# The first block of the FFN's up-projection: another order for the second token pair's sums and for the work left over at its end

## The chip, the core and the metric

One core of one Trainium2 chip runs the whole kernel as one program. The metric is the device time of that program in microseconds (us), as the median of several runs. The engines named below are PE (TensorE, the matrix products), DVE (VectorE), ACT (ScalarE), POOL (GpSimd) and SP (SyncE, which here issues nearly all DMAs). Matrix products write into PSUM, which has eight banks; DVE and ACT read the banks, POOL does not.

## The reference, cut to what matters

A trunk of two layers over 1040 tokens (16 learned ones in front of 1024) of width 1024. Layer 0 has an SSD mixer, layer 1 a stick-breaking attention. Behind each stands the same convolutional, gated FFN, and the change lies in the first half of that FFN, in both layers:

```python
def _conv_ffn(u, w_up, conv_w, conv_b, w_down):
    h = _causal_dwconv(u @ w_up, conv_w, conv_b)   # 3 taps along the tokens
    g, val = jnp.split(h, 2, axis=-1)
    return (jax.nn.silu(g) * val) @ w_down          # D_FF = 2816
```

All is float32. The kernel keeps that precision by splitting each operand into a high and a low part and making three matrix products of each one.

## The kernel before, in words

**Products.** `mm3` (line 206) issues three matmuls for one 128-row step: high by high (line 209), low by high (line 210), high by low (line 211). The up-projection takes 128 gate columns and the 128 value columns that belong to them as one *block* `b`; there are 22 blocks. The tokens form four tiles of 260 (layer 0) or 256 (layer 1), taken as two *pairs*: `block(b, 0, ...)` is the first pair, `block(b, 1, ...)` the second. For one block and one pair, gate and value columns, two halves of the width and two token tiles make a two-by-two by two-by-two product, which is done with seven products instead of eight. Each of the seven takes a *form* of the tokens (a sum or difference of token tiles and halves, made once per layer by `forms`, line 1080) and a form of the weights (made per block by `up_weights`, line 1172). One product is four steps of `mm3`, twelve matmuls.

**Where the sums stand.** Products 0 and 1 share a bank of the tag `mm` (2 banks; for the first pair of block 1 the single bank of the tag `ex`), called `x`. Products 2, 4 and 6 add up in a bank of the tag `sm` (3 banks), called `y`. Products 3 and 5 are made in a bank of `lg` (2 banks) or `ex`, called `z`. Between the products, copies of a bank into SBUF (ACT, line 1245: `p1` of `x`, `u2` of `y`, `p5` of `z`) and additions (DVE, the lambda `add`, line 1256) make the four wanted results: `x` is the gate of one tile, the value sum `v1` is the value of the other tile, `z` the gate of that one, `y` the value of the first. Product 6 adds onto `y` and has to wait until the value sum, which reads `y` with product 4 in it, is done. `conv` (line 332) makes the three taps: one ACT instruction (line 336) and two DVE instructions (line 339), the two DVE ones on one output one behind the other. `Silu` is an ACT instruction (line 1237), the product of gate and value is made on DVE (line 1241), and SP stores it (line 1242).

**The first block is special.** `enter_ffn` (line 968) makes the token forms of the first pair while the products in front still run, and those of the second pair (`rest`, the second half of `forms`) while PE already works on block 0. So block 0 is staggered: PE does the first pair's products and, between them, the second pair's products 0 and 1; products 2, 3, 5 and 4 of the second pair follow as DVE delivers the low parts of their forms (line 1103). On DVE the taps of block 0 are tied behind `first_low` (lines 1190 and 1191), the low part of block 1's first weights, and `first_low` is tied behind `last_low`, the last low part of the forms. A tie made with `behind` (line 200) only fixes the order of two instructions on one engine. What the first pair of block 0 has to do on DVE and ACT is kept in the list `late` and run when the forms are through; the second pair (`early`) runs its own at once, in the order of the source: the two additions onto `z`, the gate, product 4, the value sum `add(p5, p5, y)`, the value, and then product 6.

**Order on the engines.** Around the up-projection no order is written out by hand. A planner places the instructions by their place in the source and a simulated time, within the dependencies and the ties; tiles are taken from pools with a fixed number of buffers. From block 1 on, the two pairs go step by step side by side (`zip(s, t)`), in the order of products 0, 2, 3, 1, 4, 5, 6. Block 1's weights: `f1` (products 0 and 1) has its low part made on DVE as `first_low`, in two halves; `f2` (products 2 and 3), `f4` (product 6) and `f3` (products 4 and 5) have theirs made on POOL (line 102), in that order.

Of the kernel before, what the change touches and what calls it, by code (L numbers as in the profile page):

```python
# [10 lines left out]
AF = mybir.ActivationFunctionType  # L11
# [18 lines left out]
HB = 2  # L30
# [29 lines left out]
KF = FF // P  # L60
# [45 lines left out]
class Trunk:  # L106
# [93 lines left out]
    def behind(self, ins, other, reason):  # L200

        if other is not None:
            nosync = mybir.DependencyInfo(mybir.DependencyClass.NoSync, mybir.DependencyReason.DATA)
            self.tc.add_manual_dep(ins.ins, other.ins.name, nosync, reason=reason)

    def mm3(self, out, wh, wl, uh, ul, first, last, joins=False, tie=None):

# [124 lines left out]
    def conv(self, ps, out, n, taps, halo, wcol, bcol, between=lambda: None, tie=None):  # L332

        nc = self.nc
        o = halo - taps + 1
        nc.scalar.activation(out, ps[:, o : o + n], AF.Identity, scale=wcol(0), bias=bcol)  # L336
        between()
        for i in range(1, taps):
            ins = nc.vector.scalar_tensor_tensor(out, ps[:, o + i : o + i + n], wcol(i), out, op0=ALU.mult, op1=ALU.add)  # L339
            self.behind(ins, tie, "behind the forms")  # L340
        self.last_tap = ins
# [871 lines left out]
    def up(self, layer, w0, forms, rest, pool):  # L1213

        nc = self.nc
        tt = nc.vector.tensor_tensor
        FN = FFN[layer].tile
        N = HB + FN
        cw, cb = f"ffn_conv_w{layer}", f"ffn_conv_b{layer}"
        d = self.dp.tile([KF, P, FFN[layer].n], F32, tag=f"g{layer}", name=f"g{layer}")  # L1220

        def block(b, t, w, late=None, early=False):

            def product(i, ps, start=True):
                wh, wl, c0 = w[i]
                for k in range(KD // 2):
                    c = slice(c0 + k * P, c0 + k * P + P)
                    self.mm3(ps[:, :N], wh[:, c], wl[:, c], *forms[t][0][i][k], start and k == 0, k == KD // 2 - 1, not start, None if k else self.after_sums if late is not None and i else self.first_block if b == 1 else None)  # L1230
                return ps

            def conv(x, i, c):
                o = self.tmp("c")
                self.conv(x, o[:, :FN], FN, 3, HB, lambda q: self.par(cw, (KF * i + b) * 3 + q), self.par(cb, KF * i + b), tie=self.first_low if early or late is not None else None)
                if i == 0:
                    nc.scalar.activation(o[:, :FN], o[:, :FN], AF.Silu)
                return o

            def done(g, v, j):  # L1240
                self.last_up = tt(g[:, :FN], g[:, :FN], v[:, :FN], op=ALU.mult)
                nc.sync.dma_start(d[b, :, FN * j : FN * j + FN], g[:, :FN])

            def copy(ps, s):
                nc.scalar.activation(s[:, :N], ps[:, :N], AF.Copy)  # L1245
                return s

            def gate():
                made.update(g0=conv(x, 0, 0))

            def value():
                if late is not None:
                    self.behind(add(p5, p5, u3), self.first_low, "behind the forms")
                made.update(v1=conv(v1, 1, 1))

            add = lambda o, x, y: tt(o[:, :N], x[:, :N], y[:, :N], op=ALU.add)  # L1256
# [12 lines left out]
            u2 = copy(y, s2)  # L1269
            yield  # L1270
            s3, s4 = pair(late is not None)
            z = product(3, (self.ex if next(turn) else self.lg)("p"))
            p5 = copy(z, s3)
            if early:
                yield
                z = product(5, self.sm("p"))
                yield
                for f in (u2, p5):
                    self.behind(add(z, z, f), self.first_low, "behind the forms")
                gate()  # L1280
            else:
                add(z, z, u2)
                yield
                product(1, x, False)
                run(gate)
                yield
            product(4, y, False)
            if early:
                add(p5, p5, y)
                v1 = p5  # L1290
            elif late is None:
# [6 lines left out]
            if not early:  # L1298
                product(5, z, False)
            run(lambda: done(conv(z, 0, 1), made["v1"], 2 * t + 1))  # L1300
            yield
            product(6, y, False)
            run(lambda: done(made["g0"], conv(y, 1, 0), 2 * t))
            yield

        turn = chain((0, 0, 0, 0), cycle((1, 0, 0)))
        for b in range(KF):
            made = second if b == 1 else self.up_weights(layer, b, pool)
            w = list(made)[-1] if b else w0
            late = [] if b == 0 else None  # L1310
            s, t = block(b, 0, w, late), block(b, 1, w, early=b == 0)
            if b:
                for _ in zip(s, t):
                    pass
            else:
# [798 lines left out]
```

## Time and profile before

| | |
|---|---|
| time, median of 3 runs | 2847.6 us (2846.33 to 2847.69) |
| the profiled execution's own time | 2845.67 us |
| its span, first to last instruction | 2844.0 us |
| PE, DVE, ACT, POOL busy | 99%, 70%, 55%, 55% of the span |
| PE's granted clock, mean | 0.997 |
| entrance of the up-projection, layer 0 | from about 827 us (first product) to about 880 us (last product of block 1) |
| entrance of the up-projection, layer 1 | the same steps, about 1316.6 us later |

Times in the trace are counted from the span's first instruction. A row of the timeline shows the start, the duration, the engine, the source line, the operation, what it writes and reads, how many instructions are merged into the row, and, in brackets, how long the engine stood idle before it and what ended that. Matmuls overlap, so a matmul's duration is longer than the distance to the next one; the distance is the pace. The granted clock is 1.00 at full speed.

### The profile page before, as it was taken

The numbers are of one execution on the slowest core, as the hardware profiler recorded it, in microseconds if no ns is written. First come the engines' busy times: TensorE is split into PE (matmuls) and PEld (weight loads), VectorE is DVE, ScalarE is ACT, GpSimd is POOL, SyncE is SP. The second block draws the span as 40 slices with busy tenths as digits, with TensorE's granted clock in tenths as the row PEclk, the third lists the DMA queues.
The fourth block names the chain that finished last, engine by engine and source line by source line (L and its number), as shares of the span: only waits on it lengthen the run. The fifth ranks groups of instructions, "written<-read, shape, count | busy, mean of one in ns | idle before, by whom it ended". The sixth has DMA issues, their size and how long they took to land.

```text
span 2844.0 us, 56386 instructions
## 1 busy us (share of the span) xinstructions
PE 2803.4 (99%) x21239; PEld 2687.8 (95%) x21239; DVE 2001.7 (70%) x3922; ACT 1554.4 (55%) x2983; POOL 1552.3 (55%) x2144
## 2 busy tenths in 40 slices
PE   8999999999999999999999999999999999999998
PEld 7999999999999999999999999999898999999888
DVE  5676666668486565657886888888758565656776
ACT  5555454543255555555335777777636555555433
POOL 2365555553528777767763121111354787876881
PEclk9999999999999999999999999999999999999999
DMA  4333333343412222235142222222542222225331
GB/s 120 86 113 112 102 85 125 116 137 102 116 68 92 81 77 81 77 120 179 53 149 79 78 66 73 82 70 57 173 145 82 83 75 82 75 83 185 112 104 67
DMA packets 141740, 281.77 MB, mean 99 GB/s; under 512 B 16308, under 2 KB 71741, under 8 KB 141469
## 3 DMA queue, kind: packets, MB, share of 16 engines
q1 hardware_dynamic: 135844, 267.01, 29.6%
q0 software_dynamic: 2048, 6.49, 0.6%
q10 hardware_dynamic: 3576, 4.67, 0.5%
q8 instruction: 168, 2.75, 0.4%
q14 instruction: 104, 0.84, 0.1%
HBM read 207.79 MB, written 55.42 MB: 93 GB/s over the span
## 4 chain that ended last, share of the span: by engine, by line
PE 89%; DVE 7%; ACT 2%; issue 1%; POOL 0%; DMA 0%; DVEq 0%; ACTq 0%; SPq 0%; POOLq 0%
PE p L209 10%; PE p L211 10%; PE p L210 10%; PE acc L209 8%; PE acc L211 8%; PE acc L210 8%; PE pj L209 7%; PE pj L210 7%; PE pj L211 7%; DVE kp L1713 2%; PE po L1759 2%; PE lg L1702 2%; PE wT L1736 2%; PE y L815 1%; PE S L804 1%
## 5 line engine op out<-in xcount | busy, mean ns | idle before, releaser
L102 POOL TENSOR_TENSOR wl<-w,wh 128x256 fp32r<-128x256 f32 x760 | 679.3, 924 | 333.6 <-ACT wh L196 213.4
L209 PE MATMUL pj<-uh,wh 128*128 128x348 f32 (+2 forms) x1536 | 501.5, 327 | 3.8 <-DVE xbc L339 1.6
L210 PE MATMUL pj<-ul,wh 128*128 128x348 f32 (+2 forms) x1536 | 495.2, 322 | 0.2 <-DVE ul L320 0.2
L211 PE MATMUL pj<-uh,wl 128*128 128x348 f32 (+2 forms) x1536 | 492.0, 320 | 0.0
L339 DVE SCALAR_TENSOR_TENSOR c<-p,params,c 128x260 f32<-128x260 f32 (+1 forms) x700 | 325.9, 482 | 132.1 <-ACT c L336 129.0
L210 PE MATMUL p<-bl,fh 128*128 128x262 f32 (+1 forms) x1408 | 399.4, 284 | 1.7 <-DVE bl L1103 1.6
L211 PE MATMUL p<-bh,fl 128*128 128x262 f32 (+1 forms) x1408 | 399.9, 284 | 0.0
L209 PE MATMUL p<-bh,fh 128*128 128x262 f32 (+1 forms) x1408 | 399.6, 284 | 0.0
L102 POOL TENSOR_TENSOR fl<-x,fh 128x256 fp32r<-128x256 f32 x352 | 259.3, 770 | 219.1 <-ACT fh L1186 219.1
L209 PEld LDWEIGHTS pj<-uh,wh 128*128 128x128 f32 x1536 | 288.8, 188 | 8.3 <-DVE qs L1654 3.6
L209 PE MATMUL p<-bh,wh 128*128 128x262 f32 (+1 forms) x1040 | 295.7, 284 | 0.0
L210 PE MATMUL p<-bl,wh 128*128 128x262 f32 (+1 forms) x1040 | 294.7, 283 | 0.0
L211 PE MATMUL p<-bh,wl 128*128 128x262 f32 (+1 forms) x1040 | 294.7, 283 | 0.0
L210 PEld LDWEIGHTS pj<-ul,wh 128*128 128x128 f32 x1536 | 289.5, 188 | 1.7 <-DVE ul L320 0.6
L211 PEld LDWEIGHTS pj<-uh,wl 128*128 128x128 f32 x1536 | 289.0, 188 | 0.1
L210 PEld LDWEIGHTS p<-bl,fh 128*128 128x128 f32 x1408 | 266.9, 190 | 4.4 <-DVE bl L1103 4.1
L209 PEld LDWEIGHTS p<-bh,fh 128*128 128x128 f32 x1408 | 266.8, 190 | 0.1
L211 PEld LDWEIGHTS p<-bh,fl 128*128 128x128 f32 x1408 | 265.9, 189 | 0.0
L336 ACT ACTIVATE c<-p,params 128x260 f32<-128x260 f32 (+1 forms) x350 | 195.0, 559 | 79.2 <-DVE p L1256 53.1
L210 PE MATMUL acc<-gl,wh 128*128 128x260 f32 (+1 forms) x672 | 214.2, 320 | 0.0
L211 PE MATMUL acc<-gh,wl 128*128 128x260 f32 (+1 forms) x672 | 213.4, 319 | 0.0
L1256 DVE TENSOR_TENSOR p<-p,ft 128x262 f32<-128x262 f32 (+1 forms) x174 | 75.9, 436 | 192.2 <-ACT ft L1245 132.3
(340 smaller groups left out, 7556.0 us busy)
## 6 DMA issues: line engine op xcount, KB each, us to landing
w<-in_w_up SPq DMA_DIRECT2D x88, 512.0 KB
w<-in_w_down SPq DMA_DIRECT2D x44, 512.0 KB
w<-in_w_in SPq DMA_DIRECT2D x40, 512.0 KB
E<-ea_d SPq DMA_DIRECT2D x32, 464.0 KB
D<-acs_d SPq DMA_DIRECT2D x32, 420.5 KB
g<-c SPq DMA_DIRECT2D x88, 130.0 KB
g<-c SPq DMA_DIRECT2D x88, 128.0 KB
b<-g SPq DMA_DIRECT2D x16, 520.0 KB
```

Of the source, the lines that this page charges most:

```text
L102: done.append(eng.tensor_tensor(out[:, c], x[:, c], y[:, c], op=op))
L209: self.behind(mm(out, wh, uh, start=first, stop=False, skip_group_check=joins), tie, "behind the sums of squares")
L210: mm(out, wh, ul, start=False, stop=False, skip_group_check=joins)
L211: self.last_mm = mm(out, wl, uh, start=False, stop=last, skip_group_check=joins)
L336: nc.scalar.activation(out, ps[:, o : o + n], AF.Identity, scale=wcol(0), bias=bcol)
L339: ins = nc.vector.scalar_tensor_tensor(out, ps[:, o + i : o + i + n], wcol(i), out, op0=ALU.mult, op1=ALU.add)
L804: nc.tensor.matmul(ps, bk[:n], xde[:n].rearrange("p h d -> p (h d)"), start=True, stop=True)
L1256: add = lambda o, x, y: tt(o[:, :N], x[:, :N], y[:, :N], op=ALU.add)
L1702: nc.tensor.matmul(ps[:nt, a, :m], part[:, c0 : c0 + nt], ks[a][:, s0 : s0 + m], start=x == 0, stop=x == 1)
L1713: nc.vector.tensor_tensor_scan(rev, rev, self.one[:nt].to_broadcast([nt, m + 1]), init, ALU.mult, ALU.mult)
L1736: nc.tensor.transpose(pt[:ns, x * CB : x * CB + nt], bt[:nt, a, x * CB : x * CB + ns], self.ident[:nt, :nt])
L1759: nc.tensor.matmul(po[64 * a : 64 * a + 64, t0:n], v[: CH[c][1], c, 64 * a : 64 * a + 64], wt[a][q][: CH[c][1], r, t0:n], start=x == 0, st ...
```

## The change

Four things, all in `up` and all for block 0 and block 1 alone; the instructions and the arithmetic stay the same, and only their order and one buffer change.

1. The second pair of block 0 now puts its leftovers into a list as well (`late` is a pair of lists). Its value sum goes into a buffer of its own, `s4` (`add(v1, p5, y)`), is tied directly behind the forms' last low part and becomes the new `last_low`; `first_low` is therefore tied behind it. Product 6 follows at once, ahead of all taps of block 0.
2. The second pair's two additions onto `z`, its gate, value and both ends move to the leftovers. The `Silu` of the gate in `x` moves, in both pairs, from the gate's step to the step that finishes that tile (`soften` in `first_done`).
3. Block 1 makes products 0 and 1 of both pairs ahead of product 2 (four products in the two banks `ex` and `mm`), and its first three steps are tied one behind the other on PE.
4. The leftovers of block 0 are placed behind block 1's product 0, in this order (pair, step): the first pair's gate between the two pairs' product 0; then the first pair's first end, the second pair's gate and first end, the first pair's value and second end, the second pair's value and second end.

```diff
+                if b == 1 and i < 3:
+                    self.first_block = self.last_mm
                 return ps
...
+                return soften(o) if i == 0 and soft else o
+
+            def soften(o):
+                nc.scalar.activation(o[:, :FN], o[:, :FN], AF.Silu)
                 return o
...
-            if early:
+            if early or b == 1:
                 product(1, x, False)
                 yield
...
-                for f in (u2, p5):
-                    self.behind(add(z, z, f), self.first_low, "behind the forms")
-                gate()
+                product(4, y, False)
+                v1 = s4
+                self.last_low = self.behind(add(v1, p5, y), self.last_low, "behind the forms")
+                product(6, y, False)
+                self.first_block = self.last_mm
+                late += [gate, value, second_done, first_done]
+                yield
+                return
...
+            def first_done():
+                if late is not None:
+                    soften(made["g0"])
+                done(made["g0"], conv(y, 1, 0), 2 * t)
...
+            def second_done():
+                if early:
+                    for f in (u2, p5):
+                        self.behind(add(z, z, f), self.first_low, "behind the forms")
+                done(conv(z, 0, 1), made["v1"], 2 * t + 1)
...
+                next(t)
                 second = self.up_weights(layer, 1, pool)
                 next(second)
-                while late:
-                    for f in late[:2]:
-                        f()
-                    del late[:2]
-                    next(t, None)
-                for _ in t:
-                    pass
+            else:
+                s, t = block(b, 0, w), block(b, 1, w)
+                if b == 1:
+                    next(s)
+                    late[0][0]()
+                    next(t)
+                    for i, n in ((0, 3), (1, 0), (1, 3), (0, 1), (0, 2), (1, 1), (1, 2)):
+                        late[i][n]()
+                for _ in zip(s, t):
                     pass
-                self.first_block = self.last_mm
```

More of the change, by code (lines that the diff above doesn't have):

```diff
@@ L204, in behind @@
             self.tc.add_manual_dep(ins.ins, other.ins.name, nosync, reason=reason)
+        return ins
     def mm3(self, out, wh, wl, uh, ul, first, last, joins=False, tie=None):
@@ L1230, in product, with conv @@
                     self.mm3(ps[:, :N], wh[:, c], wl[:, c], *forms[t][0][i][k], start and k == 0, k == KD // 2 - 1, not start, None if k else self.after_sums if late is not None and i else self.first_block if b == 1 else None)
+                if b == 1 and i < 3:
+                    self.first_block = self.last_mm
                 return ps
-            def conv(x, i, c):
+            def conv(x, i, c, soft=True):
                 o = self.tmp("c")
-                self.conv(x, o[:, :FN], FN, 3, HB, lambda q: self.par(cw, (KF * i + b) * 3 + q), self.par(cb, KF * i + b), tie=self.first_low if early or late is not None else None)
-                if i == 0:
-                    nc.scalar.activation(o[:, :FN], o[:, :FN], AF.Silu)
+                self.conv(x, o[:, :FN], FN, 3, HB, lambda q: self.par(cw, (KF * i + b) * 3 + q), self.par(cb, KF * i + b), tie=self.first_low if b == 0 else None)
+                return soften(o) if i == 0 and soft else o
+            def soften(o):
+                nc.scalar.activation(o[:, :FN], o[:, :FN], AF.Silu)
                 return o
@@ L1248, in gate @@
             def gate():
-                made.update(g0=conv(x, 0, 0))
+                made.update(g0=conv(x, 0, 0, late is None))
+            def first_done():
+                if late is not None:
+                    soften(made["g0"])
+                done(made["g0"], conv(y, 1, 0), 2 * t)
             def value():
-                if late is not None:
+                if late is not None and not early:
                     self.behind(add(p5, p5, u3), self.first_low, "behind the forms")
                 made.update(v1=conv(v1, 1, 1))
+            def second_done():
[3 more added lines that the diff above has]
+                done(conv(z, 0, 1), made["v1"], 2 * t + 1)
             add = lambda o, x, y: tt(o[:, :N], x[:, :N], y[:, :N], op=ALU.add)
@@ L1270, in block @@
             yield
-            s3, s4 = pair(late is not None)
+            s3, s4 = pair(late is not None and not early)
             z = product(3, (self.ex if next(turn) else self.lg)("p"))
@@ L1277, in block @@
                 yield
-                for f in (u2, p5):
-                    self.behind(add(z, z, f), self.first_low, "behind the forms")
-                gate()
-            else:
-                add(z, z, u2)
+                product(4, y, False)
[4 more added lines that the diff above has]
+                late += [gate, value, second_done, first_done]
                 yield
+                return
+            add(z, z, u2)
+            yield
+            if b != 1:
                 product(1, x, False)
-                run(gate)
-                yield
+            run(gate)
+            yield
             product(4, y, False)
[L1288 to L1291, printed above, removed]
+            if late is None:
                 add(x, p5, y)
@@ L1297, in block @@
             yield
-            if not early:
-                product(5, z, False)
-            run(lambda: done(conv(z, 0, 1), made["v1"], 2 * t + 1))
+            product(5, z, False)
+            run(second_done)
             yield
             product(6, y, False)
-            run(lambda: done(made["g0"], conv(y, 1, 0), 2 * t))
+            run(first_done)
             yield
@@ L1309, in up @@
             w = list(made)[-1] if b else w0
[L1310 to L1313, printed above, removed]
-                    pass
-            else:
+            if b == 0:
+                late = [], []
+                s, t = (block(b, i, w, late[i], i == 1) for i in range(2))
                 next(rest)
```

## The prediction

> **What bounds the kernel now.** I read the head of the page first: how long the span is and which engine fills it.
>
> ```profile
> span 2844.0 us, 56386 instructions
> PE 2803.4 (99%) x21239; PEld 2687.8 (95%) x21239; DVE 2001.7 (70%) x3922; ACT 1554.4 (55%) x2983; POOL 1552.3 (55%) x2144
> ```
>
> PE is busy for 2803.4 of 2844.0 us, so only some 40 us of idle PE can be won anywhere. The second view is the table of PE's waits over the whole span (what waited, for what, us in total, times, longest):
>
> ```profile
> PE p L209 <- DVE ft L1256: 10.2, 2, 5.1
> ```
>
> It heads that table, and it is the change's own place. L209 is the first matmul of a step, and `ft` from line 1256 is the value sum of the second pair, `add(p5, p5, y)`: twice, once per layer, 5.1 us each. The third view is PE's timeline around the first of these:
>
> ```profile
> 851.46 0.29 PE L211 MATMUL p<-bh,fl 128*128 128x262 f32 x1
> 856.86 0.56 PE L209 MATMUL p<-bh,f 128*128 128x262 f32 x1 [5.11 <-DVE ft L1256]
> ...
> 860.05 0.29 PE L211 MATMUL p<-bh,wl 128*128 128x262 f32 x1
> ...
> 861.28 0.28 PE L209 MATMUL p<-bh,wh 128*128 128x262 f32 x1
> ...
> 862.73 0.28 PE L209 MATMUL p<-bh,fh 128*128 128x262 f32 x1
> ```
>
> The last matmul of product 4 starts at 851.46 and ends at 851.75; product 6 (its weights are called `f` in block 0) starts at 856.86. Behind the hole the pace is bad too: 14 distances from 856.86 to 860.05 are 3.19 us, 0.228 each, while the 12 of the second pair's product 0 of block 1, 861.28 to 862.73, are 1.45 us, 0.121 each. Layer 1 repeats it:
>
> ```profile
> 2173.43 0.55 PE L209 MATMUL p<-bh,f 128*128 128x258 f32 x1 [5.11 <-DVE ft L1256]
> ...
> 2177.63 0.28 PE L210 MATMUL p<-bl,wh 128*128 128x258 f32 x1
> ```
>
> From 2173.43 to 2177.63 lie 19 distances in 4.20 us; at the 0.121 of the rows above they take 2.30. The granted clock (column PEclk, the last but two) says why:
>
> ```profile
> 856.86:860.10 3.24, 3.24 (x15) 3.24 (x16) 3.24 (x7) 3.23 (x7) 3.24 (x6) 0.51 0.42 131
> 2173.43:2177.60 4.17, 4.17 (x19) 4.17 (x20) 4.17 (x9) 4.16 (x9) 4.17 (x7) 0.50 0.50 156
> 800.00:850.00 50.00, 49.09 (x365) 46.77 (x363) 45.60 (x121) 27.81 (x73) 0.14 (x2) 1.00 0.13 50
> ```
>
> It is 0.51 and 0.50 behind the holes and 1.00 in the 50 us that lead up to the first. So one hole costs 5.11 us and the slow stretch behind it.
>
> **What DVE does in the hole.** The fourth view is DVE's timeline, with the reason for the hole:
>
> ```profile
> 850.90 1.32 DVE L1103 TENSOR_TENSOR bl<-ft,bh 128x524 fp32r<-128x524 f32 x2 [0.20 <-ACT bh L1102]
> 852.13 1.82 DVE L1190 TENSOR_TENSOR wl<-w,wh 128x512 fp32r<-128x512 f32 x2
> 853.88 0.48 DVE L339 SCALAR_TENSOR_TENSOR c<-p,params,c 128x260 f32<-128x260 f32 x1
> 854.27 0.90 DVE L1256 TENSOR_TENSOR p<-p,p 128x262 f32<-128x262 f32 x2
> 855.09 0.47 DVE L339 SCALAR_TENSOR_TENSOR c<-p,params,c 128x260 f32<-128x260 f32 x1
> 855.49 0.42 DVE L1256 TENSOR_TENSOR p<-p,ft 128x262 f32<-128x262 f32 x1
> 855.82 0.56 DVE L339 SCALAR_TENSOR_TENSOR c<-p,params,c 128x260 f32<-128x260 f32 x1
> 856.30 0.41 DVE L1256 TENSOR_TENSOR ft<-ft,p 128x262 f32<-128x262 f32 x1
> ...
> 865.29 0.42 DVE L1256 TENSOR_TENSOR p<-p,ft 128x262 f32<-128x262 f32 x1
> ```
>
> The forms' last two low parts end at 852.22. Then come `first_low` (852.13, two halves), a tap of the first pair's gate, two sums (the first pair's value sum and the second pair's first addition onto `z`), the second tap, the other addition onto `z`, one more tap, and only at 856.30 the sum that product 6 waits for. Its operands were there: product 4 ended at 851.75, and the copy `p5` (quoted below at 849.95) long before. DVE itself never pauses; the order alone makes the hole.
>
> **Step 1, the value sum directly behind the forms.** The sum takes DVE's place at 852.13 instead of 856.30, at the same cost (0.41 us). PE follows 0.15 us behind its end (856.30 + 0.41 = 856.71, start 856.86). So product 6 starts at 852.13 + 0.41 + 0.15 = 852.69: 4.17 us earlier. Layer 1 by the same rows:
>
> ```profile
> 2167.50 1.30 DVE L1103 TENSOR_TENSOR bl<-ft,bh 128x516 fp32r<-128x516 f32 x2 [0.21 <-ACT bh L1102]
> 2168.72 1.81 DVE L1190 TENSOR_TENSOR wl<-w,wh 128x512 fp32r<-128x512 f32 x2
> ```
>
> 2168.72 + 0.41 + 0.15 = 2169.28 against 2173.43: 4.15 us earlier. The hole left in layer 0 is 0.94 us (851.75 to 852.69); layer 1 repeats it. Do they still slow the clock? The nearest row is a hole of 0.80 us in the stretch at clock 1.00:
>
> ```profile
> 844.07 0.39 PE L210 MATMUL p<-bl,fh 128*128 128x262 f32 x1 [0.80 <-DVE bl L1103]
> ```
>
> The matmul behind it is 0.10 longer than the usual one (0.39 for 0.29), and the stretch as a whole has the full clock. So I take the slow stretch as gone: 3.19 − 14 × 0.121 = 1.50 us in layer 0 and 4.20 − 2.30 = 1.90 us in layer 1, less 0.10 each for that one longer matmul, 1.4 and 1.8. If it stays in full, 3.2 us of the gain are lost; that is the other bound. Gain of step 1: 4.17 + 1.4 + 4.15 + 1.8 = 11.5 us.
>
> What the sum pushes back: `first_low` by 0.41 us. Its two halves (1.82 us together) then end at about 853.5 and 854.4. Block 1's product 0 reads the first half at 852.69 + 1.45 = 854.14, product 1 the second half from 857.0 on. Both are covered, the tighter one by 0.6 us. If the sum came 0.6 us later than I take it, that cover would still hold, since product 6 moves with it.
>
> **Steps 2 to 4, what is late next.** PE would run without a break: product 6 from 852.69, then one product each 1.45 us: product 0 of the pairs at 854.14 and 855.59, product 1 at 857.04 and 858.49, product 2 at 859.94 and 861.39, product 3 at 862.84 and 864.29. Each needs a bank, its copies and its weights. In the old run all of this came 5 us later with the same DVE and ACT work under way, so the price may lie here.
>
> Banks. Product 0 of the second pair needs the bank of the first pair's gate, so both its taps, which are tied behind `first_low`. The first tap starts at 852.13 + 0.41 + 1.75 = 854.29. With nothing between, the second ends at 854.29 + 0.39 + 0.48 = 855.16, and PE goes on at 855.31, in time. With two other instructions between, as in the rows now (853.88 to 855.56, 1.68 us), it ends at 855.97 and PE loses 0.53 us. Between the two I take 0.3. Product 2 needs the `y` banks, each freed by two more taps: eight taps and two multiplications of about 0.45 us put behind 854.29 end at about 858.8, ahead of 859.94 and 861.39. Of the `z` banks the first pair's is wanted at 862.84, three or four DVE instructions later. DVE's whole leftover list is now 853.88 to 865.29, 11.4 us, its order decides.
>
> Copies. The second big price is on ACT. Product 1 adds onto the bank of product 0, which `p1` must have copied:
>
> ```profile
> 849.95 0.39 ACT L1245 ACTIVATE ft<-p 128x262 f32<-128x262 f32 x1
> ...
> 854.86 1.06 ACT L336 ACTIVATE c<-p,params 128x260 f32<-128x260 f32 x2 [1.06 <-DVE p L1256]
> 855.94 1.28 ACT L1237 ACT_TABLE_LOAD   x1
> 857.23 0.42 ACT L1237 ACTIVATE c<-c 128x260 f32<-128x260 f32 x1
> ...
> 862.35 0.37 ACT L1245 ACTIVATE ft<-p 128x262 f32<-128x262 f32 x1
> ```
>
> In the old run PE had finished the first pair's product 0 of block 1 at about 861.4 and its copy (`ft<-p`) started at 862.35, 0.9 us later. With that distance the copy starts at 855.75 + 0.9 = 856.65 and ends at 857.04: just in time. If the table load for `Silu` (1.28 us) and one `Silu` (0.42) are put ahead of it at the moment it becomes possible, it ends at 857.8, and product 1 is 0.9 us late with the handover. A load started earlier costs nothing. I take 0.2. Steps 2 and 4 cost so 0.5 us per layer, bounds 0 and 1.4 (0.53 + 0.9); the sum for two layers is 1.0 us, bounds 0 and 2.8.
>
> The Trainium skill ("ScalarE: Activation LUTs", "What ACT_TABLE_LOAD costs") puts a switch of tables at about 2.66 us, a load of 1283 ns and a drain of 1380 ns. The trace shows the load of 1.28 us, directly between the end of the taps' instruction at 855.92 and the `Silu` at 857.23, and no drain. With the skill's figure the late copy would cost 1.4 us more per layer, an estimate, and the forecast below would be some 2.8 us higher.
>
> Weights. POOL makes the low parts of `f2`, `f4`, `f3` one behind the other; these are the rows of `f4` and `f3`:
>
> ```profile
> 856.06 1.60 POOL L102 TENSOR_TENSOR wl<-w,wh 128x256 fp32r<-128x256 f32 x2
> 857.62 3.37 POOL L102 TENSOR_TENSOR fl<-x,fh 128x256 fp32r<-128x256 f32 x4
> ```
>
> `f2` is ready where `f4` begins, at 856.1, and wanted at 859.94, `f3` is ready at 861.0 and wanted at 864.29 + 1.45 = 865.74: covered by 3.9 and 4.7 us. Block 2's weights (DVE's `first_low` frees the buffer of their load 0.4 us later) have block 1's 14 products, 20 us, as cover. SP's stores follow the multiplications, and no engine of the chain waits for them. These edits I put at nothing.
>
> **The sum.** 2845.67 (the profiled execution) − 11.5 + 1.0 = 2835.2 us. That execution lies 1.9 us below the median of the runs, 2847.6, so the forecast for the median is 2837.1, rounded 2837. With the bounds: residual stalls 0 gives 2836.1, all of them 2838.9, the slow clock kept on top 2842.1.
>
> **The rivals.**
>
> *The stall moves to block 1's banks.* If DVE's planner order frees the first `y` bank only at the end of the leftover list, product 2 waits from 859.94 until 854.29 + 11.4 = 865.7, 5.8 us, and the clock falls again (1.4 to 1.8 us): about 7.4 us per layer against a gain of 5.75. A half of the list, 5.7 us from 854.29, would end on time. For it: the planner has interleaved chains of taps before (853.88 to 856.30). Against it: the source puts the taps that free `y` second and fourth in the list. The likely middle case, product 2 late by 2 to 4 us, gives 2841 to 2846; the full one 2851. I put the case at 2845.
>
> *Slower: the copies at the end of ACT's list.* ACT works in order, so one conversion that waits for DVE holds up the copies behind it. If `p1` stands behind all leftovers of block 0 on ACT, and these behind DVE's list, it runs at about 865.7 and ends at 866.1; product 1, wanted at 857.04, loses 9.2 us, and the clock 1.6 more: 10.8 per layer against 5.75, so 2847.6 + 10 = 2858. It gets slower by 0.2% from about 7 us of lateness in each layer (7 + 1.6 − 5.75 = 2.85), a copy that ends at about 864. For it: in the old run the copy at 862.35 does stand behind the list of conversions. Against it: in the source the copy stands ahead of the list, and it is possible 6 us before the list ends.
>
> *The change doesn't do what it says.* In the waits of the first entrance the weight load of product 6 is put down to ACT:
>
> ```profile
> PEld p L209 <- ACT c L336: 5.3, 1, 5.3
> ```
>
> Were the conversions on ACT the true cause, an earlier sum alone would win nothing. But the conversion ends at 855.92 (854.86 + 1.06), 0.9 us before PE starts, and the DVE sum 0.15 us before. That, or a planner that undoes the order elsewhere, would give 2847.6.
>
> **How the numbers follow.** The forecast's case, no new stall over 1.4 us a layer, gets 0.68, the moved stall 0.19, the slower case 0.07, no effect 0.06. A difference of under 0.2%, 5.7 us, can hardly be told from no change for this kernel; so faster means below 2841.9, slower above 2853.3. The forecast's case is faster in nearly all of its range (2835 to 2842), and a quarter of the moved stall's is too: 0.67 + 0.05 = 0.72. Slower is 0.07 and the far end of the moved stall, 0.02: 0.09. The rest, 0.19, is the same. The predicted time is 2837; the range, 2834 to 2847, leaves out the slower case, the upper part of the moved stall and a little below (up to 2 us, if the planner's new order also shortens other small waits).
>
> **What would show it.** In the changed profile the entry of PE waiting for line 1256 should fall from 10.2 to about 2 us; the sum should be the DVE row directly ahead of `first_low`; product 6 should start some 1 us after product 4; the granted clock should stay at 1.00 through the entrance. Step 2 to 4 are wrong if PE shows waits of over 1 us for ACT line 1245 (copies) or for DVE line 339 (taps) within 12 us behind product 6. The prediction as a whole is wrong if these together exceed 5 us per layer, or if time is lost in another part of the kernel by a new order.

## The result, and the profile after

The changed kernel takes 2841.67 us in the median of 16 runs (2840.84 to 2842.83), the kernel before in the same comparison 2847.43 us (16 runs, 2846.33 to 2849.34): the ratio is 0.998 with a 95% interval of 0.9972 to 0.9987. That is 5.8 us less, where the forecast was 10.6 us (2847.6 to 2837). The time lies inside the forecast range, which says little, since that range (2834 to 2847) reaches from more than the full gain to nearly none. It is also below 2841.9, the prediction's bound for "faster", but only by 0.2 us, less than the runs scatter: on which side of the bound it fell is luck. A second set of runs gave 2841.62 us (2840.94 to 2842.15).

The head of the page of the changed kernel; its execution took 2841.43 us:

```profile
span 2839.6 us, 56382 instructions
PE 2803.0 (99%) x21239; PEld 2686.9 (95%) x21239; DVE 2003.8 (71%) x3922; ACT 1553.1 (55%) x2983; POOL 1546.7 (54%) x2144
```

The span is 4.4 us shorter and PE's busy time only 0.4 us shorter: what is gone is idle time of PE. PE's waits over the whole span (who waited for whom: us in total, times, longest) show where, and also what is new:

```profile
PE p L210 <- DVE ft L1272: 3.7, 2, 1.9
...
PE p L210 <- DVE c L340: 1.5, 1, 1.5
...
PE p L210 <- ACT wh L1187: 1.2, 2, 0.6
```

(All lines have moved: `mm3` is now lines 210 to 212, the taps line 340, `first_low` line 1191, the sums line 1272, the copies line 1250.) The old entry of 10.2 us for the value sum has become 3.7, not 2, and two entries stand behind it that the entrance did not have: a wait for taps and a wait for the high part of a weight. PE's timeline shows them in their places, layer 0 first, then layer 1:

```profile
851.33 0.29 PE L212 MATMUL p<-bh,fl 128*128 128x262 f32 x1
853.48 0.36 PE L210 MATMUL p<-bh,f 128*128 128x262 f32 x1 [1.86 <-DVE ft L1272]
...
858.06 0.36 PE L210 MATMUL p<-bh,wh 128*128 128x262 f32 x1
...
860.94 0.28 PE L212 MATMUL p<-bh,wl 128*128 128x262 f32 x1
861.80 0.39 PE L210 MATMUL p<-bh,wh 128*128 128x262 f32 x1 [0.58 <-ACT wh L1187]
862.03 0.28 PE L211 MATMUL p<-bl,wh 128*128 128x262 f32 x1
862.39 0.39 PE L210 MATMUL p<-bh,wh 128*128 128x262 f32 x1
...
2165.85 0.28 PE L212 MATMUL p<-bh,fl 128*128 128x258 f32 x1
2167.98 0.36 PE L210 MATMUL p<-bh,f 128*128 128x258 f32 x1 [1.85 <-DVE ft L1272]
2172.58 0.36 PE L210 MATMUL p<-bh,wh 128*128 128x258 f32 x1 [1.49 <-DVE c L340]
2176.29 0.39 PE L210 MATMUL p<-bh,wh 128*128 128x258 f32 x1 [0.58 <-ACT wh L1187]
```

Product 6 follows product 4 after 1.86 us instead of 5.11, not after 0.94. Behind it comes the first pair's product 0, then the second pair's (858.06 and 2172.58), then two matmuls at 861.80 and 862.03 that do not belong here: they are the first of block 2's product 0, which the planner has pulled ahead, and they wait for block 2's weights. The second pair's product 1 starts only at 862.39; without a break it would have been at 860.94 + 0.12 = 861.06, and since the two matmuls would have come later anyway (0.24 us), 1.1 us are lost.

The granted clock (last column but two) is slow behind the hole in layer 0 and full behind the same hole in layer 1:

```profile
853.48:857.12 3.64, 3.64 (x17) 3.64 (x18) 3.64 (x7) 1.67 (x3) 3.64 (x5) 0.53 0.09 30
...
2167.98:2172.00 4.02, 3.11 (x24) 2.90 (x24) 4.02 (x8) 1.94 (x4) 4.02 (x5) 1.00 0.19 53
```

DVE's timeline around layer 0's hole says why it is 1.86 us and what the second pair's product 0 waits for:

```profile
851.67 1.32 DVE L1104 TENSOR_TENSOR bl<-ft,bh 128x524 fp32r<-128x524 f32 x2 [1.11 <-ACT bh L1103]
852.91 0.42 DVE L1272 TENSOR_TENSOR ft<-ft,p 128x262 f32<-128x262 f32 x1
853.24 2.37 DVE L1191 TENSOR_TENSOR wl<-w,wh 128x512 fp32r<-128x512 f32 x2
855.53 1.27 DVE L340 SCALAR_TENSOR_TENSOR c<-p,params,c 128x260 f32<-128x260 f32 x3
856.72 0.80 DVE L1272 TENSOR_TENSOR p<-p,p 128x262 f32<-128x262 f32 x2
857.44 1.66 DVE L340 SCALAR_TENSOR_TENSOR c<-p,params,c 128x260 f32<-128x260 f32 x4
```

The sum stands where it was to stand, directly ahead of `first_low`. But DVE itself stood idle for 1.11 us ahead of the forms' last two low parts, for ACT; before, that pause was 0.20. And between the first tap of the first pair's gate (the first of the three at 855.53) and its second (the first of the four at 857.44) lie four other instructions, two taps and two sums; the second tap ends at about 857.9, and the second pair's product 0, which needs that bank, starts at 858.06. ACT's timeline shows the reason for the pause, and behind it the copies:

```profile
850.08 1.03 ACT L337 ACTIVATE c<-p,params 128x260 f32<-128x260 f32 x2
850.98 1.19 ACT L1103 ACTIVATE bh<-ft 128x524 fp32r<-128x524 f32 x2
...
859.09 1.28 ACT L1242 ACT_TABLE_LOAD   x1
860.38 0.42 ACT L1242 ACTIVATE c<-c 128x260 f32<-128x260 f32 x1
860.71 1.04 ACT L1187 ACTIVATE wh<-w 128x1024 fp32r<-128x1024 f32 x1
861.65 0.41 ACT L1242 ACTIVATE c<-c 128x260 f32<-128x260 f32 x1
861.96 0.37 ACT L1250 ACTIVATE ft<-p 128x262 f32<-128x262 f32 x1
```

Two leftover conversions (850.08, 1.03 us) stand ahead of the forms' last high parts (850.98). With the second pair's gate on the list of leftovers, the planner finds them possible at that moment and takes them. Further down, `Silu`, block 2's weights and another `Silu` stand ahead of the second pair's copy `p1` at 861.96, for which product 1 waits.

### The profile page after: what moved, and what is told of

The parts are those of the page before. It is cut to its first block, busy times and chain, and to the rows that moved or that the text cites. A ratio compares the mean times of both kernels' runs of the same rounds, so it can differ in the third digit from the quotient of the medians.

```text
span 2839.6 us, 56382 instructions
## 1 busy us (share of the span) xinstructions
PE 2803.0 (99%) x21239; PEld 2686.9 (95%) x21239; DVE 2003.8 (71%) x3922; ACT 1553.1 (55%) x2983; POOL 1546.7 (54%) x2144
## 4 chain that ended last, share of the span: by engine, by line
PE 90%; DVE 5%; ACT 3%; issue 1%; POOL 0%; DMA 0%; DVEq 0%; ACTq 0%; POOLq 0%
PE p L210 10%; PE p L212 10%; PE p L211 10%; PE acc L210 8%; PE acc L212 8%; PE acc L211 8%; PE pj L210 8%; PE pj L211 7%; PE pj L212 7%; PE lg L1719 2%; PE wT L1753 2%; PE po L1776 2%; DVE kp L1730 1%; PE y L816 1%; PE S L805 1%
## 5 line engine op out<-in xcount | busy, mean ns | idle before, releaser
L210 PE MATMUL acc<-gh,wh 128*128 128x260 f32 (+1 forms) x672 | 210.7, 320 | 0.1
```

The costliest lines, as they stand in the source:

```text
L210: self.behind(mm(out, wh, uh, start=first, stop=False, skip_group_check=joins), tie, "behind the sums of squares")
```

## The experiments

Every run is read in the same three stretches: from the start of the span to the last matmul of product 4 in layer 0, from there to the last matmul of product 4 in layer 1, and from there to the end of the span. The second stretch holds layer 0's entrance, the third layer 1's, and nothing else in them moved by more than a few tenths, unless said. The medians have the ratio to the kernel before on the same chip, with its 95% interval. The sets of runs were made on different chips, on which the kernel before had medians from 2846.5 to 2847.4 us, so a difference of under 1 us between two rows from different sets says little by itself.

| kernel | median, us | ratio | to layer 0's product 4 | from it to layer 1's | from there to the end |
|---|---|---|---|---|---|
| before | 2847.43 | | 851.46 | 1316.58 | 675.96 |
| before, again | 2846.46 (one run) | | 851.02 | 1317.30 | 676.28 |
| changed | 2841.67 | 0.998 (0.9972 to 0.9987) | 851.33 | 1314.52 | 673.75 |
| changed, again | 2841.62 | 0.9982 (0.9972 to 0.9991) | 850.95 | 1314.39 | 673.76 |
| E1 sum alone | 2841.55 | 0.9982 (0.9973 to 0.9991) | 851.87 | 1316.78 | 673.75 |
| E2 old product order | 2840.78 | 0.9979 (0.9969 to 0.9989) | 851.55 | 1314.10 | 673.45 |
| E3 conversions behind the forms | 2843.69 | 0.999 (0.9981 to 1.0) | 851.73 | 1317.42 | 672.65 |
| E4 gate's taps first | 2841.58 | 0.9981 (0.9972 to 0.9991) | 851.93 | 1313.49 | 674.18 |
| E5 copies first | 2839.73 | 0.9976 (0.9966 to 0.9986) | 851.12 | 1313.51 | 672.67 |
| E6 = E3 + E4 + E5 | 2834.79 | 0.9958 (0.9943 to 0.9973) | 850.85 | 1311.27 | 670.08 |
| E6, again | 2834.42 | 0.9954 (0.994 to 0.9967) | 850.58 | 1311.28 | 670.14 |
| E7 = E4 + E5 | 2839.28 | 0.9977 (0.9967 to 0.9986) | 852.08 | 1312.79 | 672.93 |
| E8 = E6 with the old product order | 2839.78 | 0.9973 (0.9963 to 0.9984) | 852.28 | 1315.17 | 671.15 |

The first stretch, which no edit touches, differs by up to 1.7 us between executions, but by at most 0.4 us between those of one chip; the other two are the ones to read.

**E1, step 1 alone.** The kernel before with the value sum and product 6 of the second pair put directly behind the forms; leftovers and block 1 as before.

```diff
                 z = product(5, self.sm("p"))
                 yield
+                product(4, y, False)
+                v1 = s4
+                self.last_low = self.behind(add(v1, p5, y), self.last_low, "behind the forms")
+                product(6, y, False)
+                yield
...
-            product(6, y, False)
+            if not early:
+                product(6, y, False)
...
+                next(t)
                 second = self.up_weights(layer, 1, pool)
```

> The kernel before with step 1 alone: the value sum directly behind the forms' last low part, product 6 behind it, everything else (order of the leftovers, block 1's product order, Silu with the gate) as before. Here ACT has no leftover conversions ahead of the forms' last high parts. Theory 'order' (what PE wins at product 6 is lost again where the order on DVE and ACT gives banks and copies back): the hole ahead of product 6 is about 1.0 us, not 1.86, but block 1's product 2 comes 2.9 us behind product 0 while the taps of the first bank y stand near the end of DVE's list, so PE waits 2 to 5 us there or at the copies; the time is 2842 to 2847. Rival 'the sum is all' (steps 2 to 4 give nothing): no such wait, time at or below the changed kernel's 2841.7.

It measured 2841.55 us (2839.47 to 2844.08), the time of the whole change. PE's timeline of E1 has the hole that step 1 forecast, and then another one:

```profile
853.10 0.36 PE L210 MATMUL p<-bh,f 128*128 128x262 f32 x1 [0.95 <-DVE ft L1257]
861.83 0.59 PE L210 MATMUL p<-bh,wh 128*128 128x262 f32 x1 [2.63 <-ACT wh L1187]
...
2169.88 0.36 PE L210 MATMUL p<-bh,f 128*128 128x258 f32 x1 [0.94 <-DVE ft L1257]
2177.91 0.39 PE L210 MATMUL p<-bh,wh 128*128 128x258 f32 x1 [2.03 <-ACT ft L1246]
```

And the 4 us behind the second hole of layer 0, with the granted clock:

```profile
861.83:865.83 4.00, 4.00 (x18) 4.00 (x19) 3.02 (x8) 2.70 (x8) 4.00 (x6) 0.50 0.21 70
```

So step 1 does what it was costed at: the hole is 0.95 and 0.94 us. Much of what it wins is taken back 8 to 9 us later by waits for ACT: the copies and block 2's weights come in their old places, and the clock falls there instead, in layer 1 too (0.61). These are the waits of theory 'order' (2 to 5 us), while the time is just inside what the rival allowed (at or below 2841.7); so neither came out whole. (The profiled execution is the slowest of E1's ten, 2844.08 us.) Steps 2 to 4 together win nothing on top: they make the second wait smaller and the first hole larger.

**E2, step 3 undone.** The changed kernel with block 1's products in the order 0, 2, 3, 1 again.

```diff
-            if early or b == 1:
+            if early:
                 product(1, x, False)
                 yield
...
-            if b != 1:
-                product(1, x, False)
+            product(1, x, False)
```

> The changed kernel with block 1's products in the order 0, 2, 3, 1 again (step 3 undone, leftovers still in the new order). Theory 'order': the bank of the first pair's y is free about 0.4 us behind the bank that product 0 of the second pair waits for, so product 2 hardly waits, and the copy that makes product 1 of the second pair 1.1 us late per layer is no longer urgent: up to 2 us faster than the changed kernel, 2839.5 to 2841.7. Rival 'four products first is what hides the leftovers': product 2 waits 1 to 4 us per layer, 2843 to 2848.

2840.78 us, 0.9 less than the changed kernel (on another chip), and 0.4 and 0.3 us less in the two stretches. The waits of 1 to 4 us that the rival expected are not there; the longest for a tap is 0.55 us. Four products in two banks first are worth nothing in the changed kernel. What they are worth in a better one is E8's question.

**E3, the conversions behind the forms.** The changed kernel, with the leftovers' conversions on ACT tied behind the forms' last high part.

```diff
-        nc.scalar.activation(out, ps[:, o : o + n], AF.Identity, scale=wcol(0), bias=bcol)
+        self.behind(nc.scalar.activation(out, ps[:, o : o + n], AF.Identity, scale=wcol(0), bias=bcol), high, "behind the forms")
...
-    ... tie=self.first_low if b == 0 else None)
+    ... tie=self.first_low if b == 0 else None, high=self.last_high if b == 0 else None)
```

> The changed kernel with ACT's conversions of block 0's leftovers (line 337) tied behind the forms' last high part. Theory 'order': DVE no longer waits 1.11 us for that high part, the whole chain last low part, sum, first_low, taps comes 0.8 to 0.9 us earlier, product 6's hole falls from 1.86 to 1.0 us and product 0 of the second pair starts 0.85 us earlier: 2840.0 (1.7 us below the changed kernel). Rival 'the clock decides' (the slow stretch behind the hole sets block 1's start in layer 0): with a hole of 1.0 us the slow stretch of layer 0 goes and it wins more, up to 3 us.

2843.69 us, 2.0 more than the changed kernel, where both readings expected less. The hole ahead of product 6 falls to 0.66 and 0.52 us, so the conversions had made it longer. But PE's timeline has others in its place:

```profile
857.95 0.36 PE L210 MATMUL p<-bh,wh 128*128 128x262 f32 x1 [2.11 <-DVE c L340]
...
2167.72 0.39 PE L210 MATMUL p<-bh,fh 128*128 128x258 f32 x1 [2.64 <-ACT p L1250]
```

In layer 0 the second pair's product 0 starts 6.2 us behind product 4's last matmul where it started 6.7 us behind it: of the 1.2 us that the hole is shorter, 0.5 are left, since ACT makes the conversions later and DVE takes two sums ahead of the first tap. And in layer 1 the planner now sets one copy (`p`) behind the forms and the weights on ACT, and product 4 itself waits 2.64 us for it; that alone is most of the 2.9 us by which the middle stretch is longer.

**E4, the gate's taps first.** The changed kernel, with the first pair's gate done whole before any other leftover: all of them are tied behind its second tap.

```diff
                     late[0][0]()
+                    self.first_low = self.last_tap
                     next(t)
```

> The changed kernel with both taps of the first pair's gate directly behind one another on DVE and all other leftovers behind them. Theory 'order': the second tap comes up 1.6 to 1.9 us earlier (it now has four to five other instructions ahead of it); in layer 1 the wait of 1.49 us of product 0 for it goes; in layer 0 the slow clock makes product 0 of the first pair end just when the tap ends now, so the gain there is 0 to 0.3 us unless the clock stays up: 2839.9 to 2841.4. Rival 'POOL beside DVE': the slow part is first_low itself (2.37 us instead of 1.82), the taps then still come late and nothing is won.

2841.58 us: no change. This is the rival's time but not its reason: `first_low` still takes 2.37 us, and yet PE no longer waits for the taps. It waits for the next link instead, block 2's weights:

```profile
861.42 0.39 PE L210 MATMUL p<-bh,wh 128*128 128x262 f32 x1 [0.96 <-ACT wh L1187]
...
2174.81 0.39 PE L210 MATMUL p<-bh,wh 128*128 128x258 f32 x1 [2.33 <-ACT wh L1187]
```

**E5, the copies first.** The changed kernel, with the leftovers' `Silu` and the high part of block 2's first weights tied behind the copies `p1` of block 1.

```diff
+                if b == 2 and not own and n == D:
+                    self.behind(high, self.copied, "behind the copies")
...
             def soften(o):
-                nc.scalar.activation(o[:, :FN], o[:, :FN], AF.Silu)
+                self.behind(nc.scalar.activation(o[:, :FN], o[:, :FN], AF.Silu), self.copied if b == 0 else None, "behind the copies")
...
             p1 = copy(x, s1)
+            if b == 1:
+                self.copied = self.last_copy
```

> The changed kernel with ACT's Silu of block 0's leftovers and the high part of block 2's first weights tied behind the copies of block 1's product 0. Theory 'order': the second pair's product 1 of block 1 starts without the wait of 0.58 us for block 2's weights and of 0.4 us for its copy, 1.1 us earlier per layer: 2839.5 (2.2 us below the changed kernel). Rival 'banks': the next bank (y of the first pair, freed by taps and a Silu that now come later) takes the wait over, and the time is 2841 to 2843.

2839.73 us, 1.9 less than the changed kernel; 1.0 and 1.1 us less in the two stretches. That is the size of the late product 1 (1.1 us a layer). The wait for `wh` is gone; the hole (1.88 and 1.86 us) and the wait for the taps (1.44 and 1.49 us) stay.

**E6, all three.** The edits of E3, E4 and E5 on the changed kernel.

> All three ties together: conversions behind the forms' last high part, gate taps first, Silu and block 2's weights behind the copies. Theory 'order': the hole ahead of product 6 is 1.0 us, product 0 and 1 of block 1 start without a wait of over 0.3 us, 2836 to 2838 (the forecast's 2837.1 for the change itself). If the slow stretch comes back in a layer, 1.5 us more for each. Rival 'POOL beside DVE': first_low stays long and the second pair's product 0 still waits about 1 us per layer, 2838.5 to 2840.

> E6 once more, unchanged, in more rounds. If its order is what makes it fast, 2834 to 2836 us again, with one hole of 0.6 to 0.7 us in each layer, product 4 to the 120th matmul behind product 6's start in 15.9 to 16.1 us, and no slow clock. If E6 was a lucky execution, 2838 us or more, with a wait of over 1 us back in one of the layers.

2834.79 us, and in the second set, of five runs, 2834.42 us (2833.84 to 2834.53). That is 6.9 to 7.2 us less than the changed kernel, where the three edits alone gave +2.0, −0.1 and −1.9, and it is below the 2836 to 2838 that theory 'order' gave, with a shorter hole than its 1.0 us. The rows of E6, PE's and DVE's timelines and PE's clock over both entrances:

```profile
851.80 0.36 PE L210 MATMUL p<-bh,f 128*128 128x262 f32 x1 [0.67 <-ACT wh L1187]
...
2163.06 0.36 PE L210 MATMUL p<-bh,f 128*128 128x258 f32 x1 [0.65 <-ACT wh L1187]
```

```profile
848.77 2.54 DVE L1104 TENSOR_TENSOR bl<-ft,bh 128x524 fp32r<-128x524 f32 x4
851.23 0.42 DVE L1274 TENSOR_TENSOR ft<-ft,p 128x262 f32<-128x262 f32 x1
851.56 2.20 DVE L1191 TENSOR_TENSOR wl<-w,wh 128x512 fp32r<-128x512 f32 x2
```

```profile
850.00:866.00 16.00, 15.33 (x124) 14.89 (x123) 15.96 (x32) 12.99 (x25) 14.66 (x18) 1.00 0.33 119
2162.00:2178.00 16.00, 15.35 (x125) 14.90 (x124) 15.96 (x32) 12.94 (x26) 15.38 (x19) 1.00 0.35 125
```

The forms' low parts run without a pause, the sum follows, and the hole of 0.67 us is PE's only one of over 0.2 us in the 15 us behind product 4 (0.65 in layer 1; 0.68 and 0.67 in the second set). (The profile names ACT there; but product 6 reads nothing of `wh`, and the sum's end at 851.65 and the usual 0.15 us give 851.80.) The clock is full throughout. Against the kernel before, the two stretches are 5.3 and 5.9 us shorter, 11.2 together.

**E7, without the conversions' tie.** E4 and E5 together.

> The changed kernel with the edits of E4 and E5 together, without E3's (the leftover conversions stay ahead of the forms' last high parts). Theory of one chain: the hole behind product 4 stays 1.8 to 1.9 us in each layer, but product 0 of the second pair waits for nothing (gate's taps first) and neither does product 1 (copies first), so that each layer gains about 2.7 us on the changed kernel, E6's gain less E3's share of it: 2841.6 - 5.4 = 2836.2 us, between 2835 and 2838. Rival: the conversions' place is what the other two ties need, and without it each hands the time on to the next link as E4 and E5 did alone: 2839 us or more, with a wait of 1 us or more ahead of product 0 or product 1 in the waits of TensorE.

2839.28 us (nine of the ten runs from 2839.10 to 2839.90, one at 2848.69, of which there is no trace): the rival's time with the chain theory's picture. No wait of 1 us stands ahead of product 0 or 1 of the second pair in PE's timeline, only the hole itself:

```profile
854.25 0.36 PE L210 MATMUL p<-bh,f 128*128 128x262 f32 x1 [1.88 <-DVE ft L1274]
...
2167.00 0.36 PE L210 MATMUL p<-bh,f 128*128 128x258 f32 x1 [1.84 <-DVE ft L1274]
2173.30 0.39 PE L210 MATMUL p<-bh,wh 128*128 128x258 f32 x1 [0.24 <-ACT ft L1252]
```

```profile
854.25:858.25 4.00, 3.96 (x30) 3.78 (x31) 3.96 (x7) 2.06 (x4) 4.00 (x5) 1.00 0.16 50
2167.00:2171.00 4.00, 4.00 (x23) 4.00 (x24) 3.96 (x7) 1.67 (x3) 4.00 (x5) 0.64 0.19 41
```

The price was wrong, then, not the mechanism. E6 is 1.5 and 2.8 us a layer better than E7: 1.2 of each is the hole (1.88 less 0.67, 1.84 less 0.65), and in layer 1 most of the rest is the slow clock behind it, 0.64 over 4 us where layer 0 has 1.00: the 24 matmuls from product 6 to the second pair's product 0 take 4.40 us there and 3.20 in layer 0. I had given the conversions' tie too little: taken alone it had lost time, and taken last it is worth 4.5 us (2839.28 less 2834.79).

**E8, step 3 undone in E6.** E6 with block 1's products in the order 0, 2, 3, 1, by E2's edit.

> E6 (all three ties) with block 1's products in the order 0, 2, 3, 1 of the kernel before. If four products in two banks first is worth nothing, as E2 showed without the ties, 2833.9 to 2834.8 us, with the same hole of 0.6 to 0.7 us in each layer and no other wait of TensorE. Rival: with the gate's taps done first, it is now the y bank that comes late, and the product order hides it: then product 2 of the second pair waits 1 to 2 us for a tap of DVE in each layer and the time is 2836 to 2839 us.

2839.78 us, 5.0 more than E6, beyond the upper end of the rival's range. PE's timeline has small waits for taps, and a larger one ahead of layer 1's product 4:

```profile
858.37 0.36 PE L210 MATMUL p<-bh,fh 128*128 128x262 f32 x1 [0.41 <-DVE c L340]
860.69 0.36 PE L210 MATMUL p<-bh,fh 128*128 128x262 f32 x1 [0.61 <-DVE c L340]
...
2166.03 0.39 PE L210 MATMUL p<-bh,fh 128*128 128x258 f32 x1 [2.65 <-ACT p L1252]
```

```profile
2165.08 0.62 ACT L1187 ACTIVATE wh<-w 128x512 fp32r<-128x512 f32 x1
2165.60 0.37 ACT L1252 ACTIVATE p<-p 128x258 f32<-128x258 f32 x1
```

The middle stretch is 3.9 us longer than E6's: 2.65 for the copy `p`, which ACT makes behind the weights' high part as in E3, and 1.25 with the waits for taps (0.41 + 0.61); the last stretch is 1.1 longer, with waits for taps of 0.20 and 0.79. So the product order itself is worth 1.1 to 1.25 us a layer here, the rival's mechanism at the low end of its price, and the other 2.65 us are an order of ACT that came along with it. Why the planner sets that copy late in E3 and E8 and not in E6 wasn't tried.

**Both kernels again.** Unchanged, beside E5 and E6.

> The changed kernel once more, to see which of its readings repeat. Theory 'order': the chain from the last low part to the second pair's product 0 of block 1 is 6.4 us in both layers again whatever the clock does, and the slow stretch behind the hole of 1.86 us may come in either layer, both or none, without changing the time by more than 0.5 us. Rival 'the clock decides': the time moves by 1.5 us with each slow stretch. 2841.7 expected.

> The kernel before once more. Both holes of 5.1 us and a slow stretch of 3 to 4.5 us behind each; if one hole is followed by full clock at once, the time of that run is 1.5 to 2 us lower. 2847.4 expected.

2841.62 and 2846.46 us. The kernel before has both its holes again (5.11 and 5.08 us), with a clock of 0.50 behind each. The changed kernel's repeat settles what the slow clock costs there. Behind the hole of layer 1 the clock was full the first time (1.00) and slow now:

```profile
2167.47:2171.47 4.00, 4.00 (x22) 4.00 (x23) 4.00 (x8) 1.93 (x4) 4.00 (x5) 0.62 0.16 52
```

And the stretch from layer 1's product 4 to the end is 673.75 us with the full clock and 673.76 with the slow one. The chain from the last low parts to the second pair's product 0 is 6.4 us in both layers of both executions, as theory 'order' had it.

## Why the prediction was right, and where it was wrong

**What bounds the kernel** was read rightly. The order on DVE alone made the hole, and E1 shows it: with the sum moved and nothing else, it falls from 5.11 to 0.95 and 0.94 us, against 0.94 forecast. The rival that the change doesn't do what it says, with the weight load's wait for ACT as evidence, falls with it.

**Step 1, product 6 earlier by 4.17 and 4.15 us: mis-sized, 3.25 and 3.26.** The sum's place and its 0.42 us were right. The step took DVE's place at 852.13 as given, the end of the forms' low parts. Step 2 of the change, which puts the second pair's gate among the leftovers, gave ACT two conversions (1.03 us) to do ahead of the last high parts, and these delay DVE by a pause of 1.11 us in place of 0.20. E3 shows it: with the conversions tied behind, the hole is 0.66 us. I priced what the moved work waits for and not what it now stands in front of. It cost 0.9 us a layer.

**Step 1, the slow stretch gone, 1.4 and 1.8 us: it stayed in layer 0, but its price was wrong in both.** In layer 0 the clock is slow for 3.64 us behind the hole of 1.86 us; with the hole that I had forecast it stays full, as E1 shows. But in the changed kernel PE's pace decides nothing just behind product 6. From the start of product 6 to the second pair's product 0 it is 4.58 us in layer 0 with the slow clock (853.48 to 858.06) and 4.60 in layer 1 with the full one (2167.98 to 2172.58). E5 has the full clock in both layers (1.00), 4.60 us in both, and now shows PE's wait for the taps in layer 0 as well:

```profile
853.28 0.36 PE L210 MATMUL p<-bh,f 128*128 128x262 f32 x1 [1.88 <-DVE ft L1274]
...
857.88 0.36 PE L210 MATMUL p<-bh,wh 128*128 128x262 f32 x1 [1.44 <-DVE c L340]
```

So the slow clock only fills a wait: DVE's chain sets the second pair's product 0, not PE's pace. The two executions of the changed kernel, 673.75 and 673.76 us, agree. In E7, where that chain is short, the slow clock does cost 1.2 us (4.40 for 3.20), most of the 1.3 us by which layer 1's stretch differs more from E6's than layer 0's.

**Steps 2 to 4, 0.5 us a layer, bounds 0 and 1.4: mis-sized, about 2.6 in each layer.** The banks: I had two instructions between the gate's taps, there are four, and the first tap starts 2.29 us behind `first_low` where I had 1.75. Where PE does not wait, product 6 and the first pair's product 0 take 3.0 us (851.80 to 854.83 in E6); here it is 4.6, so the second tap costs 1.55 us a layer, over the bound of 0.53. In layer 1, 1.49 us of it show as PE's wait; in layer 0 it is hidden under the slow clock. The copies: 1.1 us a layer against a bound of 0.9, for the cause that was named (table load and `Silu` ahead of `p1`) and one that was not: block 2's weights are also ahead of it, and two matmuls of block 2, which the planner pulled ahead, wait for them. E5 takes both away and wins 1.0 and 1.1 us. The sentence that put block 2's weights at nothing, with 20 us of cover, was wrong for that reason: the cover was counted in the order of the source.

The rows behind these points add up. Of the forecast 10.5 us in the profiled execution, the longer hole takes 1.8, and banks and copies take 2.1 more than forecast in each layer: 6.0 us, and 10.5 − 6.0 = 4.5, where the spans differ by 4.4.

**The signs.** Of what the prediction named to look for, the sum does stand directly ahead of `first_low`. PE's wait for it is 3.7 us for both layers instead of 2, product 6 comes after 1.86 us instead of 1, and the clock does not stay at 1.00. The wait of 1.49 us for the taps is the sign that was to show steps 2 to 4 wrong, and it does.

**The rivals.** The stall that moves to block 1's banks happened in small, about 1.5 us a layer and not 2 to 4, and at the bank of product 0, not at that of product 2. The slower case did not: the first pair's `p1` is made at 858.19, long ahead of the point from which it was to decide (a copy that ends at about 864), and the second pair's ends at 862.33. On the table load the Trainium skill ("ScalarE: Activation LUTs", "What ACT_TABLE_LOAD costs") has a drain of 1380 ns beside the load; the `Silu` at 860.38 follows the load's 859.09 + 1.28 = 860.37, so here again the trace shows none, and the measurement decides.

**What the sum was worth.** E6 has the forecast's picture, one hole of under 1 us, a full clock and no other wait of over 0.2 us, and its two stretches are 11.2 us shorter than before's, near the 11.5 that step 1 was put at. As far as these executions show, the forecast was thus right about what the hole is worth and wrong in taking it that this change gets it.

## What to carry to other kernels

Waits around one place form a chain: taking away the longest hands its time to the next link, and an edit that wins nothing alone (E3 loses 2.0 us) may be worth 4.5 us once the others are in. Where a planner orders the work, moving a piece to a list frees not only its old place: ask on each engine what the planner will now find possible earlier, and in front of what it will stand. A tie that only fixes the order can undo this (E6), but a single tie can also lose time (E3). And before pricing a slow clock, ask whether PE's pace sets anything in that stretch.

## What the runs showed of the hardware

**The clock behind a short hole.** Over all profiles, the mean granted clock of the 4 us behind a hole of PE was 1.00 behind every hole of up to 1.6 us in these entrances, slow (0.50 to 0.60) behind the four of 5.1 us in the two executions of the kernel before, and either behind those between: holes of 1.84 to 1.88 us were followed by 0.57 to 0.66 in 6 of 12 and by 1.00 in the other 6, those of 2.0 to 2.65 us in 3 of 6. One kernel shows both at one place (layer 1 of the changed kernel: 1.00 and 0.62). Nor does the slow pace start where the hole ends: in E7's layer 1 the first nine matmuls behind the hole still go at full pace (2167.00 to 2168.02), and only then come distances of 0.22 us instead of 0.12. The slow stretches lasted from 3.2 us (E1, layer 1) to 6.1 us (E1, layer 0). The Trainium skill ("TensorE: Matmul & The Clock Gate", "What's actually happening") tells of a free-running window of some 3.4 us, and says that the moment at which the clock rises at a kernel's start depends on where in it the first matmul falls. Stretches of about one to two such windows and the chance fit it, though nothing here shows the window itself. The rule that it gives in "HAM oscillation — how this bites in real kernels", no idle gaps of more than about 3.4 us, is not enough here: half of the holes of 1.9 us, well under it, were followed by the slow clock.

**DVE beside POOL.** The halves of `first_low`, the same subtraction of 128x512, took 0.69 and 1.22 us before, 1.22 both in the changed kernel and 1.05 and 1.22 in E6. POOL begins its subtractions at 852.41, 853.19 and 851.34 in these three, 0.28 us into the first half before, and ahead of it in the other two. The Trainium skill ("Advanced Engine Details and Errata", "GPSIMD Details") says that POOL shares a read and a write interface with DVE and conflicts with DVE instructions that have two inputs in SBUF, as this subtraction has; the rows fit, but no run was made to tell this from another cause. It adds about 0.5 us ahead of the first tap, which my step 2 did not have.
